# Shifting the start of matmul operand tiles by 128 to 416 bytes in a two-layer hybrid decoder kernel

## The chip, the cores and the metric

The kernel runs on one core of a Trainium2 chip, as one launch. The metric is the device time of that launch in microseconds (us). Three runs of the kernel before gave 1892.44 us as their median, with 1891.72 and 1893.65 us as the ends.

## What is computed

256 tokens of width 1024 go through two layers and a final norm. In short:

```python
for l in range(2):
    sh1, sc1, g1, sh2, sc2, g2 = split(silu(c) @ w_ada[l] + b_ada[l], 6)
    h = rms_norm(x) * (1 + sc1) + sh1
    A, B, C, gates = split(h @ w_in[l])
    m = sig(gA) * (delta_net(A) @ PA) + sig(gB) * (ssd(B) @ PB) + sig(gC) * (mla(C) @ PC)
    x = x + g1 * (m @ w_out[l])
    h = rms_norm(x) * (1 + sc2) + sh2
    f = swiglu(h) if l == 0 else top2_of_8_experts(h)      # experts: 1024 -> 3584 -> 1024
    x = x + g2 * f
out = rms_norm(x) * final_norm_w
```

All weights and activations are float32.

## The kernel before

**Precision.** Every large product is made from three fp32r matmuls. A 1 MB block of weights arrives in a `raw` tile by one DMA on SP's queue (`load_raw`, L145 to L149). `chunk` (L160 to L180) splits it: ScalarE copies it to `whi` in fp32r (L170), VectorE subtracts to get the rest, `wlo` (L172). Activations are split in the same way into a high and a low part. `mm3` (L98) then issues high times high, high times low and low times high, each through `mm`, whose one line (L96) all of these matmuls carry in the profile.

In a row such as `mmt<-whi,xx` the first name behind the arrow is the moving operand (512 columns of weights, streamed) and the second the stationary one (a 128 by 128 block of activations, loaded into the array by the LDWEIGHTS of the same pair). Where a row reads `hh,whi` the two have changed parts.

**The weight ring.** `ring` (L151) hands out `whi` and `wlo` tiles of 4 KB per partition, four of each, in the pool `wp`.

**The stages.** First the mixer of layer 0 (L533 on), then the dense SwiGLU of layer 0 (L1222 on), the mixer of layer 1, and the expert stage of layer 1 (`moe`, L1310 on). Pools of a stage are opened when it begins and take the space that the stage before has left:

- `mx` holds the mixer's small tensors and 16 tiles of 2 KB (`wg`, L539 and L540, tag `w2k`). The delta rule's matrices are there, and in the output product one of the two weight halves, split into `ohi` and `olo` (the second job of `tmajor_gemms` at the end of `mixer`), and in layer 1 the half `qhi`, `qlo` of the query projection.
- `mo`, `mr` and `me` belong to the expert stage. `choose` (L1498) writes the selection matrices `Pm` into `mo`, two buffers. `gather` (L1507) multiplies the tokens `h2` by `Pm` and splits the outcome into `xx`, one tile for two experts in `me` (`[P, 2, 2, KD, P]`: expert, high or low, block of 128 features, 128 tokens). `expert` (L1551) uses it.

**One expert.** Each of the eight experts has 128 slots. `expert` runs seven blocks of 512 hidden columns: the gate product and the up product, each 8 feature blocks times 3 matmuls, so 48 matmuls of 512 columns with `xx` stationary. A block's gate and up are multiplied, turned by four transposes (`trt<-cst,sg`, L1566) and split into `act` (L1549 in the profile, since `behind` issues it). Then 14 chunks of the down weights follow, each with 12 matmuls with `act` stationary, and every second expert has the gather for the next pair in between (32 matmuls `trt<-Pm,h`). The expert's output is scaled, split into `yh` and `yl` (the latter named `sg`) and sent back to the tokens by `outer` (L1589): 8 matmuls with the transposed selection `PTm` as stationary operand, added to `xs` by VectorE (L1607). `outer` is issued two steps later, inside the next expert's first block.

**What sets the order.** The source order, and `behind`/`issue_after`, which places an instruction behind a named one in its engine's queue. Waits come from the tiles: a DMA into `raw` waits for the `wlo` subtraction that read it last, `whi` waits for the matmuls that read that ring slot last, `wlo` for `whi`, and the matmuls for both.

Of the kernel before, what the change touches and what calls it, by code (L numbers as in the profile page):

```python
# [10 lines left out]
F32 = mybir.dt.float32  # L11
# [8 lines left out]
P = 128  # L20
# [41 lines left out]
def trunk_kernel(ctx, tc, a, out, dbg=None):  # L62
# [38 lines left out]
        mm(o, ll, rh, False, stop)  # L101

    nsm = [0]

    def small(w, name, dt=F32, bufs=2):
        return cp.tile([P, w], dt, name=name, tag=name, bufs=bufs)
# [38 lines left out]
    def load_raw(src, k, n, raw=None):  # L145

        raw = raw_tile() if raw is None else raw
        last["load"] = nc.sync.dma_start(raw[:, :k * n], src)
        return raw  # L149
# [383 lines left out]
    def mixer(l, after=None):  # L533

        with tc.tile_pool(name=f"mx{l}", bufs=1, reuse_waits="tile") as mp, \
                tc.tile_pool(name=f"mb{l}", bufs=1, reuse_waits="tile", side="right") as bp, \
                tc.tile_pool(name=f"mc{l}", bufs=1, reuse_waits="tile", side="right") as qp:

            def wg(name, dt=F32):  # L539
                return mp.tile([P, 512], dt, name=name, tag="w2k", bufs=16)  # L540
# [769 lines left out]
    def moe(l):  # L1310
        with tc.tile_pool(name=f"mw{l}", bufs=1, reuse_waits="tile", side="right") as xp, \
                tc.tile_pool(name=f"mo{l}", bufs=1, reuse_waits="tile") as mp:
            for i in range(6):
                xp.tile([P, 2048], F32, name="raw", tag=f"rx{i}")

            extra.update(order=[(xp, f"rx{i}", 1) for i in (3, 4)] + [own] * 2 + [(xp, f"rx{i}", 1) for i in (2, 0, 1, 5)] + [own])
            turn[0] = 0
            ahead.extend(load_raw(w, 4, 512, shot(xp, i, "raw")) for i, w in enumerate(first_srcs[3:7]))
            ahead.extend(load_raw(w, 4, 512) for w in first_srcs[7:15])
            h2 = [mp.tile([P, NT, D], F32R, name="h2", tag="h2", bufs=2) for _ in range(2)]  # L1320
            slot = mp.tile([P, NT, NE], F32, name="slot")
            wsel = mp.tile([P, NT, NE], F32, name="wsel")
            sel = mp.tile([P, NT, NE], F32, name="sel")
            ovi = mp.tile([P, 4], I32, name="ovi")
            ovs = mp.tile([P, 3, 2, NT], F32, name="ovs")
            with tc.tile_pool(name=f"mr{l}", bufs=1, reuse_waits="tile") as rp, \
                    tc.tile_pool(name=f"me{l}", bufs=1, reuse_waits="tile") as ep:
                rest, weights = route(l, rp, h2, slot, wsel, sel)
                pair = lambda e: choose(mp, [lambda t, i=i: slot[:, t, i:i + 1] for i in (e, e + 1)])
                Pm = pair(0)  # L1330
                behind("Pm", rest)
                ready = [(x, Pm, i) for i, x in enumerate(gather(l, ep, h2, Pm, 2, True))]
                behind("xl", weights)
                late = {16: 2, 17: 3, 27: 3}
                ahead.extend(load_raw(first_srcs[i], 4, 512, shot(xp, late[i], "raw") if i in late else None)
                             for i in range(15, 28))
                row_tile[l, 5] = lambda: mp.tile([P, 512], F32, name="g2", tag="g2", bufs=2)
                ada_rows(l, 5)
                g2 = [rows[l, 10 + c] for c in range(2)]

                def after_first(c):
                    if c == 1:
                        with tc.issue_after(last["act"].ins), tc.issue_after(last["tr"].ins):
                            overflow_data(ep, slot, wsel, sel, ovi, ovs)
                def finish():

                    fw, o, f = (raw_tile() for _ in range(3))
                    nc.sync.dma_start(fw[:, :D], a["final_w"])
                    o, f = (x.rearrange("p (t n) -> p t n", t=NT) for x in (o, f))
                    for t in range(NT):  # L1350
                        rs = rms_scale(t, lambda c: o[:, t, c * 512:(c + 1) * 512])
                        for c in range(2):
                            cs = slice(c * 512, (c + 1) * 512)
                            G.tensor_mul(f[:, t, cs], xs[:, t, cs], fw[:, cs])
                        for c in range(2):
                            cs = slice(c * 512, (c + 1) * 512)
                            if c:
                                V.tensor_scalar(o[:, t, cs], f[:, t, cs], rs, None, op0=OP.mult)
                            else:
                                A.activation(o[:, t, cs], f[:, t, cs], AF.Copy, scale=rs)  # L1360
                            nc.sync.dma_start(out[t * P:(t + 1) * P, cs], o[:, t, cs])

                for e in range(NE):
                    x, Pm, i = ready.pop(0)

                    def between():
                        Pm = behind("lo", pair, e + 1)
                        ready.extend((x, Pm, i) for i, x in enumerate(gather(l, ep, h2, Pm, 2)))
                    expert(l, e, ep, xp, x, lambda t, Pm=Pm, i=i: Pm[:, t, i], lambda t, e=e: wsel[:, t, e:e + 1], g2,
                           after_first if e == 0 else None, between if e % 2 and e < NE - 1 else None)  # L1370
                stages.flush()
                finish()
                overflow(l, mp, ep, xp, h2, g2, ovi, ovs, finish)
            extra.clear()

# [37 lines left out]
    def route(l, rp, h2, slot, wsel, sel):  # L1413


        iota = cst[:, C_IOTA:C_IOTA + P]
        lgs, rs = routed["lgs"], routed["rs"]
        tap("logits", lgs)
        halves = [(t, slice(c * 512, (c + 1) * 512)) for c in range(2) for t in range(NT)]
        for t, cs in halves:  # L1420
            A.activation(h2[0][:, t, cs], xs[:, t, cs], AF.Copy, scale=rs[t])
        m8 = rp.tile([P, NT, 8], F32, name="m8")
        i8 = rp.tile([P, NT, 8], U32, name="i8")
        for t in range(NT):
            V.max(m8[:, t], lgs[:, t])
        for t in range(NT):
            V.max_index(i8[:, t], m8[:, t], lgs[:, t])
        i2 = rp.tile([P, NT, 2], F32, name="i2")
        V.tensor_copy(i2, i8[:, :, :2])
        oh = rp.tile([P, NT, 2, NE], F32, name="oh")  # L1430
        V.tensor_tensor(oh.rearrange("p t j n -> p (t j) n"), iota[:, :NE].unsqueeze(1).to_broadcast([P, 2 * NT, NE]),
                        bc(i2.rearrange("p t j -> p (t j)"), NE), op=OP.is_equal)
        chosen = V.tensor_add(sel, oh[:, :, 0], oh[:, :, 1])
        ps = sstile()
        mm(ps[:, 0:NE], cst[:, C_SU:C_SU + P], sel[:, 0], True, True)
        mm(ps[:, NE:2 * NE], cst[:, C_SU:C_SU + P], sel[:, 1], True, False)
        ins = mm(ps[:, NE:2 * NE], ones, sel[:, 0], False, True)
        with tc.issue_after(ins.ins):
            warm(pre[0][0][0], RWARM[2], mmtile)
        V.scalar_tensor_tensor(slot.rearrange("p t n -> p (t n)"), ps[:, :2 * NE], 1.0,  # L1440
                               sel.rearrange("p t n -> p (t n)"), op0=OP.add, op1=OP.mult)

        def low(i):
            t, cs = halves[i]
            V.scalar_tensor_tensor(h2[1][:, t, cs], xs[:, t, cs], rs[t], h2[0][:, t, cs].bitcast(F32), op0=OP.mult,
                                   op1=OP.subtract)
        with tc.issue_after(last["xs"].ins):
            low(0)
        with tc.issue_after(chosen.ins):
            low(1)  # L1450

        def rest():
            low(2)
            low(3)

        def weights():
            e2 = rp.tile([P, NT], F32, name="e2")
            V.tensor_sub(e2, m8[:, :, 1], m8[:, :, 0])
            A.activation(e2, e2, AF.Exp)
            w = rp.tile([P, 2, NT], F32, name="w")  # L1460
            V.tensor_scalar(w[:, 0], e2, 1.0, None, op0=OP.add)
            V.reciprocal(w[:, 0], w[:, 0])
            V.tensor_mul(w[:, 1], e2, w[:, 0])
            for t in range(NT):
                V.tensor_scalar(wsel[:, t], oh[:, t, 0], w[:, 0, t:t + 1], None, op0=OP.mult)
                V.scalar_tensor_tensor(wsel[:, t], oh[:, t, 1], w[:, 1, t:t + 1], wsel[:, t], op0=OP.mult, op1=OP.add)
        return rest, weights
# [328 lines left out]
```

## Time and profile before

| | |
|---|---|
| median of three runs | 1892.44 us (1891.72 to 1893.65) |
| the profiled execution | 1891.01 us |
| its span, first to last instruction | 1889.2 us |
| TensorE (PE) busy | 1841.5 us, 97% |
| VectorE (DVE) busy | 1602.2 us, 85% |
| ScalarE (ACT) busy | 1231.6 us, 65% |
| DMA, mean over the span | 281 GB/s |
| instructions | 25651 |

The profiled execution is one more run, 1.43 us under the median of the three. Its span leaves out 1.8 us of start and end. Matmuls are pipelined: a 512-column one is shown as lasting about 0.39 us although the next starts about 0.23 us later, so what one costs the engine is read from the distance between starts, not from its own length.

### The profile page before, as it was taken

The page shows a single profiled execution, that of the slowest core. Times are in us where ns is not written, and L with a number is a line of the kernel's source. Part 1 is how long each engine was busy: PE and PEld are TensorE (multiplying, and loading weights), DVE is VectorE, ACT ScalarE, POOL GpSimd, SP SyncE. Part 2 cuts the span into 40 slices and gives each one's busy share as a digit, 9 for nine tenths or more (in the row PEclk, how much of TensorE's full clock was granted, in tenths as well). Part 3 has the DMA queues.
Part 4 walks back from the last instruction along what each step waited for, and adds up shares of the span by engine and source line. Part 5 has one row for each costly group of instructions (what it writes and reads, how often), then busy time and mean ns, then how long its engine had stood idle before and what let it go on. Part 6 is the DMA issues. An engine that isn't in the chain of part 4 may idle for free.

```text
span 1889.2 us, 25651 instructions
## 1 busy us (share of the span) xinstructions
PE 1841.5 (97%) x9490; PEld 1545.4 (82%) x9490; DVE 1602.2 (85%) x2313; ACT 1231.6 (65%) x1599; POOL 43.3 (2%) x61
## 2 busy tenths in 40 slices
PE   8999999999999999999999999999999999999996
PEld 6899887788889998888887878878778888788785
DVE  7998788777578978877999989998898999899997
ACT  4665445644466644457777777777877777777775
POOL 0000010000000000100000000000000000000001
PEclk9999999999999999999999999999999999999998
DMA  9453457677644654758998989999899999899892
GB/s 365 160 202 131 171 198 270 235 257 263 211 144 148 221 184 173 276 204 357 340 354 331 356 313 362 363 359 349 331 352 344 354 363 367 307 357 378 336 353 84
DMA packets 75016, 530.19 MB, mean 281 GB/s; under 512 B 8578, under 2 KB 8962, under 8 KB 12548
## 3 DMA queue, kind: packets, MB, share of 16 engines
q1 hardware_dynamic: 74884, 528.49, 74.1%
q8 instruction: 76, 1.25, 0.3%
q14 instruction: 56, 0.46, 0.1%
HBM read 527.41 MB, written 1.05 MB: 280 GB/s over the span
## 4 chain that ended last, share of the span: by engine, by line
PE 87%; DVE 6%; ACT 3%; issue 2%; DMA 2%; DVEq 0%; ACTq 0%; SPq 0%
PE mmt L96 76%; PE smt L96 6%; DVE wlo L172 2%; PE sst L96 2%; PE trt L1566 1%; DVE raw L199 1%; ACT whi L170 1%; PE trt L258 1%; ACT sg L1527 1%; DMA raw<-in_ffn_w_down_dram 0%; PE trt L1073 0%; PE trt L96 0%; DMA raw<-in_w_ada_pair_dram 0%; DMA raw<-in_w_out_dram 0%; DMA raw<-in_w_ada_gate_dram 0%
## 5 line engine op out<-in xcount | busy, mean ns | idle before, releaser
L172 DVE TENSOR_TENSOR wlo<-raw,whi 128x1024 fp32r<-128x1024 f32 (+1 forms) x874 | 1043.7, 1223 | 128.1 <-ACT whi L170 107.1
L170 ACT ACTIVATE whi<-raw 128x1024 fp32r<-128x1024 f32 (+1 forms) x874 | 908.2, 1059 | 305.2 <-PE mmt L96 253.4
L96 PE MATMUL mmt<-whi,xx 128*128 128x512 f32 x1792 | 579.0, 398 | 0.0
L96 PEld LDWEIGHTS mmt<-whi,xx 128*128 128x128 f32 x1792 | 337.4, 188 | 75.0
L96 PE MATMUL mmt<-wlo,xx 128*128 128x512 f32 x896 | 357.6, 399 | 4.9 <-DVE wlo L172 4.9
L96 PE MATMUL mmt<-whi,act 128*128 128x512 f32 x896 | 281.0, 391 | 1.2 <-ACT whi L170 1.2
L96 PEld LDWEIGHTS mmt<-wlo,xx 128*128 128x128 f32 x896 | 168.8, 188 | 52.3 <-DVE wlo L172 16.4
L96 PEld LDWEIGHTS mmt<-whi,act 128*128 128x128 f32 x896 | 167.5, 188 | 36.4 <-ACT whi L170 2.5
L96 PE MATMUL mmt<-whi,hh 128*128 128x512 f32 (+2 forms) x480 | 184.0, 389 | 5.8 <-ACT hh L292 2.0
L96 PE MATMUL mmt<-whi,hl 128*128 128x512 f32 (+2 forms) x480 | 181.1, 383 | 0.5 <-DVE hl L293 0.5
L96 PE MATMUL mmt<-wlo,hh 128*128 128x512 f32 (+2 forms) x480 | 181.2, 383 | 0.0
L96 PE MATMUL mmt<-wlo,act 128*128 128x512 f32 x448 | 175.3, 391 | 1.8 <-DVE wlo L172 1.6
L199 DVE CUSTOM_DVE_ANT_0 raw<-raw,sc_b,pv 128x1024 f32<-128x1024 f32 x96 | 123.2, 1298 | 12.8 <-DMA raw<-in_w_ada_pair_dram 9.8
L96 PEld LDWEIGHTS mmt<-whi,hh 128*128 128x128 f32 x480 | 91.0, 190 | 23.7 <-ACT hh L292 2.6
L96 PEld LDWEIGHTS mmt<-whi,hl 128*128 128x128 f32 x480 | 90.7, 189 | 18.0 <-DVE hl L293 1.0
L96 PEld LDWEIGHTS mmt<-wlo,hh 128*128 128x128 f32 x480 | 90.9, 189 | 16.2 <-DVE wlo L172 0.2
L96 PEld LDWEIGHTS mmt<-wlo,act 128*128 128x128 f32 x448 | 84.1, 188 | 22.3 <-DVE wlo L172 4.4
L96 PE MATMUL mmt<-hh,whi 128*128 128x256 f32 x320 | 92.3, 290 | 0.5 <-ACT whi L170 0.5
L96 PE MATMUL mmt<-hh,wlo 128*128 128x256 f32 x320 | 90.6, 287 | 1.1 <-DVE wlo L172 1.1
L96 PE MATMUL mmt<-hl,whi 128*128 128x256 f32 x320 | 91.0, 285 | 0.0
L1549 ACT ACTIVATE act<-trt 128x512 fp32r<-128x512 f32 x56 | 33.1, 591 | 72.0 <-PE trt L1566 72.0
L1549 DVE TENSOR_TENSOR act<-trt,act 128x512 fp32r<-128x512 f32 x56 | 38.6, 689 | 33.2 <-ACT act L1549 32.7
(422 smaller groups left out, 2226.9 us busy)
## 6 DMA issues: line engine op xcount, KB each, us to landing
raw<-in_moe_w_gate_dram SPq DMA_DIRECT2D x112, 1024.0 KB, 6.0
raw<-in_moe_w_up_dram SPq DMA_DIRECT2D x112, 1024.0 KB, 6.2
raw<-in_moe_w_down_dram SPq DMA_DIRECT2D x112, 1024.0 KB, 6.9
raw<-in_w_in_dram SPq DMA_DIRECT2D x50, 1024.0 KB, 4.9
raw<-in_w_ada_pair_dram SPq DMA_DIRECT2D x32, 1024.0 KB, 5.0
raw<-in_w_ada_gate_dram SPq DMA_DIRECT2D x16, 1024.0 KB, 4.9
raw<-in_ffn_w_down_dram SPq DMA_DIRECT2D x11, 1024.0 KB, 5.5
raw<-in_ffn_w_gate_dram SPq DMA_DIRECT2D x10, 1024.0 KB, 4.9
```

Of the source, the lines that this page charges most:

```text
L96: return T.matmul(o, l, r, start=start, stop=stop, skip_group_check=True)
L170: last["hi"] = A.activation(hi[:, :m], r, AF.Copy)
L172: last["lo"] = V.tensor_sub(lo[:, :m], r, hi[:, :m].bitcast(F32))
L199: last["ada"] = V.tensor_tensor_reduce(r, r, sc_b, 1.0, pv[l][:, PP_BADA + i:PP_BADA + i + 1], OP.mult, OP.add, modc[l][:, i:i + 1])
L258: T.transpose(ps[:, j * S + t * P:j * S + (t + 1) * P], src(t, b0 + j), ident)
L1527: A.activation(tmp[:, o], ps[:, o], AF.Identity, scale=sc, bias=sh)
L1549: return trace(*args, **kw)
L1566: last["tr"] = T.transpose(ps[:, b * P:(b + 1) * P], sg[:, b * P:(b + 1) * P], ident)
```

## The change

Nothing is computed differently. A helper `gap(pool, n)` takes a tile of n bytes per partition that nobody writes or reads, and so moves whatever the pool places behind it:

```diff
+    def gap(pool, n):
+
+        pool.tile([P, n // 4], F32, name="gap", tag=f"gap{n}")
...
         with tc.tile_pool(name=f"mx{l}", bufs=1, reuse_waits="tile") as mp, \
                 tc.tile_pool(name=f"mb{l}", bufs=1, reuse_waits="tile", side="right") as bp, \
                 tc.tile_pool(name=f"mc{l}", bufs=1, reuse_waits="tile", side="right") as qp:
+
+            gap(mp, 128)
...
             ovs = mp.tile([P, 3, 2, NT], F32, name="ovs")
+            gap(mp, 224)
             with tc.tile_pool(name=f"mr{l}", bufs=1, reuse_waits="tile") as rp, \
                     tc.tile_pool(name=f"me{l}", bufs=1, reuse_waits="tile") as ep:
+                gap(ep, 160)
...
                             overflow_data(ep, slot, wsel, sel, ovi, ovs)
+                            gap(ep, 32)
```

Every engine has the same instructions in the same order with the same waits as before; only addresses differ. Where tiles begin in a partition (first buffer in bytes, and what is left modulo 256, which all buffers of a tile share):

| tile | pool | before | left | after | left |
|---|---|---|---|---|---|
| `whi`, `wlo` ring | `wp` | 59872, 76256 | 224 | the same | 224 |
| `hh`, `hl` (in the expert stage `h2`) | `hp`, `mo` | 92640, 100832 | 224 | the same | 224 |
| `act` | `mw` | 196576 | 224 | the same | 224 |
| `yh`, `yl` of the mixers | `mb` | 182240, 181216 | 224 | the same | 224 |
| mixers' 2 KB tiles (`ohi`, `olo`, `qhi`, `qlo`, the delta rule's) | `mx` | 113760 | 96 | 113888 | 224 |
| `Pm` | `mo` | 109312 | 0 | 109536 | 224 |
| `xx` | `me` | 117856 | 96 | 118240 | 224 |
| `sg` | `me` | 134240 | 96 | 134624 | 224 |
| `PTm` | `me` | 140384 | 96 | 140768 | 224 |
| `yh` of the experts | `me` | 142656 | 64 | 143072 | 224 |

The blocks that a matmul reads inside these tiles lie at multiples of 512 bytes from their start, so what is left modulo 256 holds for each of them too.

## Rows read from the trace of the kernel before

**Rows 1.** The page, busy time of the engines: us, share of the span, instructions.
```profile
PE 1841.5 (97%) x9490; PEld 1545.4 (82%) x9490; DVE 1602.2 (85%) x2313; ACT 1231.6 (65%) x1599; POOL 43.3 (2%) x61
```

**Rows 2.** The page, the chain that ended last, by engine and line.
```profile
PE mmt L96 76%; PE smt L96 6%; DVE wlo L172 2%; PE sst L96 2%; PE trt L1566 1%; DVE raw L199 1%; ACT whi L170 1%; PE trt L258 1%; ACT sg L1527 1%; DMA raw<-in_ffn_w_down_dram 0%; PE trt L1073 0%; PE trt L96 0%; DMA raw<-in_w_ada_pair_dram 0%; DMA raw<-in_w_out_dram 0%; DMA raw<-in_w_ada_gate_dram 0%
```

**Rows 3.** Stretches: the expert stage; length, PE, PEld, DVE, ACT, POOL busy, clock, DMA share, GB/s.
```profile
866.00:1869.00 1003.00, 995.12 (x4475) 805.09 (x4474) 908.17 (x929) 768.91 (x839) 2.29 (x7) 1.00 0.89 341
```

**Rows 4.** Line L96 on PE: count, shortest/median/longest ns, first and last start, forms.
```profile
L96 PE MATMUL mmt<-whi,xx x1792: 387/393/483, 865.8 to 1830.6; 128*128 128x512 f32 x200
L96 PE MATMUL mmt<-wlo,xx x896: 387/393/505, 866.1 to 1830.4; 128*128 128x512 f32 x180
L96 PE MATMUL mmt<-whi,act x896: 387/389/499, 949.7 to 1869.2; 128*128 128x512 f32 x180
...
L96 PE MATMUL mmt<-whi,yh x96: 387/389/481, 217.6 to 824.2; 128*128 128x512 f32 x96
```

**Rows 5.** Timeline of PE, one gate and up block: start, us, line, operation, tiles.
```profile
1402.33 0.40 PE L96 MATMUL mmt<-wlo,xx 128*128 128x512 f32 x1
...
1413.03 0.40 PE L96 MATMUL mmt<-whi,xx 128*128 128x512 f32 x1
```

**Rows 6.** Timeline of PE, one stretch of the down product.
```profile
1340.20 0.39 PE L96 MATMUL mmt<-whi,act 128*128 128x512 f32 x1
...
1349.72 0.39 PE L96 MATMUL mmt<-whi,act 128*128 128x512 f32 x1
```

**Rows 7.** Timeline of PE, output product of layer 1's mixer: second half, then first half.
```profile
834.85 0.40 PE L96 MATMUL mmt<-ohi,hl 128*128 128x512 f32 x1
...
839.04 0.40 PE L96 MATMUL mmt<-ohi,hl 128*128 128x512 f32 x1
...
840.21 0.39 PE L96 MATMUL mmt<-wlo,hh 128*128 128x512 f32 x1
...
843.84 0.39 PE L96 MATMUL mmt<-whi,hl 128*128 128x512 f32 x1
```

**Rows 8.** Timeline of PE, 256-column matmuls: a mixer's projection, and a gather.
```profile
560.09 0.28 PE L96 MATMUL mmt<-hh,wlo 128*128 128x256 f32 x1
...
561.53 0.28 PE L96 MATMUL mmt<-hh,wlo 128*128 128x256 f32 x1
...
1355.84 3.90 PE L96 MATMUL trt<-Pm,h 128*128 128x256 f32 x32
1359.58 0.39 PE L96 MATMUL mmt<-whi,act 128*128 128x512 f32 x1
```

**Rows 9.** Waits in the expert stage (866 to 1869): us in total, times, longest.
```profile
ACT whi L170 <- PE mmt L96: 131.7, 396, 2.7
ACT act L1549 <- PE trt L1566: 72.0, 36, 2.2
...
PEld mmt L96 <- DVE wlo L172: 20.9, 44, 1.1
...
SPq L148 <- DVE wlo L172: 806.9, 309, 9.1
```

**Rows 10.** Timeline of PE at the change from one expert to the next.
```profile
1369.64 0.40 PE L96 MATMUL mmt<-whi,xx 128*128 128x512 f32 x1
...
1381.94 0.50 PE L96 MATMUL mmt<-wlo,xx 128*128 128x512 f32 x1 [0.78 <-DVE wlo L172]
```

**Rows 11.** Timelines of PE and PEld around one late `wlo` inside a block.
```profile
1425.57 0.40 PE L96 MATMUL mmt<-wlo,xx 128*128 128x512 f32 x1
...
1428.40 0.19 PEld L96 LDWEIGHTS mmt<-wlo,xx 128*128 128x128 f32 x1 [0.30 <-DVE wlo L172]
```

**Rows 12.** Timeline of DVE: a split of `xx`, and work of one block.
```profile
1365.36 0.68 DVE L1533 TENSOR_TENSOR xx<-sg,xx 128x512 fp32r<-128x512 f32 x1
...
1388.48 3.49 DVE L172 TENSOR_TENSOR wlo<-raw,whi 128x1024 fp32r<-128x1024 f32 x3
1391.89 0.68 DVE L1549 TENSOR_TENSOR act<-trt,act 128x512 fp32r<-128x512 f32 x1
```

## The prediction

> **What bounds the kernel now.** I read the busy times first: TensorE (PE) is busy 97% of the span [rows 1], and matmuls of line L96 into `mmt` alone are 76% of the chain that ended last [rows 2]. So what a matmul costs PE counts, unless something else is late where it gets cheaper. [...]
>
> The view of line L96 by tiles shows what the change is about. The same `whi` and `wlo` ring is the moving operand in all four rows of that group, and all are 512 columns wide. With `act` or the mixers' `yh` stationary the median is 389 ns, with `xx` 393 [rows 4]. Of the four stationary tiles `xx` alone begins at another place modulo 256 than the ring (96 against 224).
>
> Since matmuls overlap, the price is the distance between starts. In one gate and up block the starts from 1402.33 to 1413.03 are 46 distances: 10.70/46 = **232.6 ns** [rows 5]. In the down product 42 distances fill 1340.20 to 1349.72: 9.52/42 = **226.7 ns** [rows 6]. The difference is 5.9 ns.
>
> That could belong to the stage and not to the place. The output product of a mixer is the control: same line, same stationary `hh` and `hl`, same PSUM use, a few us apart, and only the moving tile differs. With `ohi` and `olo` (place 96) 18 distances take 839.04 - 834.85 = 4.19 us, 232.8 ns each. With the ring (224) 16 take 843.84 - 840.21 = 3.63 us, 226.9 ns each [rows 7]. The same 5.9 ns, with the roles of the two operands exchanged. So the place of the operands matters. That it is the place modulo 256 is my reading: the dearer tiles also lie in one stretch of the partition, 113760 to 147 thousand, and the trace has no tile there at 224 that could tell the two apart.
>
> **The change part by part.** No instruction, order or wait changes, so the whole effect must come from durations.
>
> *`xx` from 96 to 224.* There are 1792 + 896 = 2688 matmuls with `xx` [rows 4]. No row shows `xx` at 224. Its price then lies between 226.7, the price with `act` at 224 in the same stage, and 232.6, no change; I take 226.7, because `act` has the same size, the same moving tiles and the same stage. Gross gain: 2688 x 5.9 ns = **15.9 us**. The worse end, a price above 232.6, is a rival below.
>
> *What of it is absorbed.* PE does not run alone. Two waits end at a time that other engines set, and PE only reaches them earlier.
> - Change of expert. DVE is behind after scaling and adding the previous output, and PE stands 0.78 us for `wlo`, having started 39 `xx` matmuls since 1369.64 [rows 10]. Their 39 x 5.9 ns = 0.23 us goes into that wait. There are seven such changes: 1.6 us.
> - Inside blocks. ACT, once it is ahead, waits in order for the four transposes, 36 times in the stage; its copies and DVE's next `wlo` come late from there, and PE's weight load waits for `wlo` 44 times [rows 9]. Such a wait ends at 1428.40, and the first matmul after the one behind the transposes began at 1425.57, 12 distances before [rows 11]. This chain has a fixed length, so 12 x 5.9 ns = 0.07 us is lost each time: 44 x 0.07 = 3.1 us.
>
> Net for `xx`: 15.9 - 1.6 - 3.1 = **11.2 us**. Where the stalls go, the late thing is always the next `wlo`. DVE can follow: three `wlo` take 1391.89 - 1388.48 = 3.41 us, 1.14 us each [rows 12], so a block of eight with two smaller operations of at most 0.68 costs DVE 8 x 1.14 + 2 x 0.68 = 10.5 us, while PE needs 48 x 226.7 ns = 10.9 us for the matmuls alone.
>
> *Mixers' 2 KB tiles from 96 to 224.* Those with 512 columns on PE are `ohi`/`olo` (48 matmuls in layer 0, 24 in layer 1) and `qhi`/`qlo` (24): 96 x 5.9 ns = **0.6 us** gained, all on PE's path at most, and nothing as the other end. The delta rule's tiles have 64 or 128 columns and were both at 96 already; for them, as for the transposes, I count nothing.
>
> *`PTm` and `yh` of the experts.* 64 matmuls, 64 x 5.9 ns = 0.4 us at most. They run in the stretch before the wait at the change of expert [rows 10], which covers them: **0**. If that cover is gone, 0.4 us more is gained.
>
> *`Pm` from 0 to 224.* Here the nearest rows speak against the change. 32 gather matmuls of 256 columns, `Pm` moving at 0 and `h2` stationary at 224, take 1359.58 - 1355.84 = 3.74 us, 116.9 ns each. The mixer's 256-column matmuls with both at 224 take (561.53 - 560.09)/12 = 120.0 ns [rows 8]. So the four gathers, 128 matmuls, may cost 128 x 3.1 ns = **0.4 us more**; the other end is nothing.
>
> *ACT and DVE on moved tiles.* DVE's split into `xx` (96) takes 0.68 us and its split into `act` (224) also 0.68 [rows 12]. I count nothing.
>
> *DMA.* No transfer moves. SP's queue waits 309 times for DVE to free a `raw` tile [rows 9], and no wait for weights from memory stands among that stage's longer ones, so the transfers are ahead of the work. At a DMA share of 0.89 [rows 3], a stage shorter by 1.1% raises it to 0.90.
>
> **Sum.** -11.2 - 0.6 + 0.4 = -11.4 us on the profiled execution's 1891.01, so 1879.6. The median of the runs, 1892.44, is 1.43 above the profiled one; by the same difference I predict **1881.0 us**. The bounds of the terms: all 15.9 arrives, with 0.6 and 0.4 on top, gives 1892.44 - 16.9 = 1875.5; the other way, twice as much absorbed (9.4) and nothing from the mixers, 1892.44 - 6.5 + 0.4 = 1886.3. A measurement of this kernel can tell 0.2%, 3.8 us, from no change.
>
> **The rivals.**
>
> *The late `wlo` takes it all in most blocks* (chance 0.08). Where ACT already waits for the transposes, the chain from there to `wlo` sets the pace of the whole block. Then 36 of 56 blocks [rows 9] gain nothing: 36 x 48 x 5.9 ns = 10.2 us lost instead of 3.1. 15.9 - 1.6 - 10.2 = 4.1 us remain, 1888.3. Against it: only 12 of the 48 distances lie between the transposes and the late `wlo` [rows 11], and ACT waits for PE to free ring tiles 396 times [rows 9], so most splits are ready early.
>
> *The place modulo 256 does nothing* (0.14): **1892.4**. The cause would be the stretch of the partition in which these pools lie, which the gaps leave as it is. For it: all tiles at the price of 232.6 are there. Against it: those at 226.7 lie below it (ring, `hh`) and far above (`act`, `yh`), which leaves no simple rule by distance. [...]
>
> *Equal places are worse* (0.04), the slower side. If two streams that begin at the same place modulo 256 met in the same piece of memory, moving `xx` onto the ring's place would add what the gathers suggest, 3.1 ns per matmul [rows 8]: 2688 x 3.1 = 8.3 us, **1900.7**. It decides against the change once the distance with `xx` exceeds 232.6 + 3.8/2.688 = 234.0 ns. Against it: ring and `act`, ring and `hh` are such equal pairs and cost 227 ns [rows 6, 7].
>
> **How the numbers follow.** The forecast, full effect with some absorbed, has 0.74. With 0.08, 0.14 and 0.04 the chances add to 1. The forecast's bounds, 1875.5 to 1886.3, and the absorbed case, 1888.3, make up 0.82; I let the range run from 1875 to 1889 and leave the other two out. Faster by over 3.8 us means below 1888.6: nearly all of the first two cases, 0.81. Within 3.8 us: the no-effect case and a remainder of the absorbed one, 0.15. Slower: 0.04.
>
> **What would show it.** Right, if the medians with `xx` fall from 393 to 389 ns and the distances to about 227 ns, those of `ohi` too, while `act` stays at 226.7; if PE's weight loads wait longer for `wlo`, by some 5 us in all; and if the expert stage ends 11 us earlier with the 866 us before it shortened by under 1 us. Gather distances near 120 ns would show the small loss. Wrong, if `xx` stays at 232.6 (the place is not it, or not this remainder), or if it falls to 227 and the stage still takes 1003 us: then the waits for `wlo` have grown by the whole 15.9 us, and DVE or ACT is the bound.

## The result, and the profile after

The changed kernel takes **1879.91 us** (median of 8 runs, 1878.59 to 1887.58) beside 1892.41 us for the kernel before (8 runs, 1889.61 to 1897.14): a ratio of 0.9939, 95% interval 0.9925 to 0.9953, so 0.6% faster. The forecast was 1881.0 us, with a range of 1875 to 1889. The profiled execution took 1882.09 us over a span of 1880.3, 2.2 us above its median.

The page, busy time of the engines, to be held against [rows 1]:

```profile
PE 1832.1 (97%) x9490; PEld 1545.1 (82%) x9490; DVE 1600.5 (85%) x2313; ACT 1231.8 (66%) x1599; POOL 42.1 (2%) x61
```

The counts are the same for every engine. PE's busy time fell by 9.4 us, that of no other engine by more than 1.7. The expert stage, same columns as [rows 3]:

```profile
866.00:1860.00 994.00, 986.42 (x4491) 805.73 (x4491) 908.02 (x931) 770.00 (x841) 2.26 (x7) 1.00 0.90 345
```

The granted clock of the stage is 1.00, as before; the DMA share went from 0.89 to 0.90. PE is still the engine that is busy nearly throughout. By tiles of line L96, the rows that answer to [rows 4], with the output product of the mixers and the `PTm` product below (count, shortest/median/longest ns, first and last start, forms):

```profile
L96 PE MATMUL mmt<-whi,xx x1792: 387/389/481, 868.0 to 1821.9; 128*128 128x512 f32 x200
L96 PE MATMUL mmt<-wlo,xx x896: 387/389/507, 868.2 to 1821.7; 128*128 128x512 f32 x180
L96 PE MATMUL mmt<-whi,act x896: 387/389/501, 950.2 to 1860.5; 128*128 128x512 f32 x180
...
L96 PE MATMUL mmt<-ohi,hh x40: 278/389/481, 314.6 to 854.1; 128*128 128x512 f32 x24, 128*128 128x256 f32 x16
...
L96 PE MATMUL smt<-yh,PTm x32: 389/389/501, 995.8 to 1864.1; 128*128 128x512 f32 x32
```

`xx` has come down from 393 to the 389 that `act` kept. From the first `xx` start to the last `act` start the stage takes 1860.5 - 868.0 = **992.5 us**, where it took 1869.2 - 865.8 = 1003.4 [rows 4]: 10.9 us less, of the 12.5 by which the medians differ.

The first 866 us say nothing at this size. In the profiled executions of this document (e2 left out, where the ring moves in the mixers too) the stage starts anywhere from 863.6 to 868.0: at 868.0 in the change and at 864.0 in the run e6 below, two kernels that issue the same work from the same places up to the gather just before it. Most of these 4.0 us come with the granted clock. Between the 2800th and the 3000th matmul (509 to 556 us) the lead of e6 grows from 1.2 to 4.0 us, and from 542 to 550 us the clock of the change is 0.57 on the mean, with 0.50 in each us from 543 to 549, where e6 has 1.00 over the whole. It had fallen by 543.27, when PE had stood idle for 2.03 us; e6, some 1.2 us ahead there, shows no fall from 542 to 550. The stretch first in the change, then in e6, columns as above:

```profile
542.00:550.00 8.00, 6.73 (x22) 6.11 (x23) 4.44 (x7) 7.71 (x16) 0.00 (x0) 0.57 0.00 1
...
542.00:550.00 8.00, 7.89 (x42) 7.13 (x43) 5.59 (x8) 7.30 (x14) 0.00 (x0) 1.00 0.00 0
```

The timeline of PE in one gate and up block shows that the new price is not one number (start, us, line, operation, tiles):

```profile
1400.96 0.39 PE L96 MATMUL mmt<-wlo,xx 128*128 128x512 f32 x1
...
1408.44 0.39 PE L96 MATMUL mmt<-wlo,xx 128*128 128x512 f32 x1
1408.67 0.39 PE L96 MATMUL mmt<-whi,xx 128*128 128x512 f32 x1
1408.90 0.60 PE L1576 MATMUL trt<-cst,sg 128*128 128x128 f32 x4
1409.26 0.48 PE L96 MATMUL mmt<-whi,xx 128*128 128x512 f32 x1
1409.57 0.40 PE L96 MATMUL mmt<-wlo,xx 128*128 128x512 f32 x1
...
1411.65 0.39 PE L96 MATMUL mmt<-wlo,xx 128*128 128x512 f32 x1
1411.88 0.61 PE L96 MATMUL mmt<-whi,xx 128*128 128x512 f32 x2
1412.33 0.39 PE L96 MATMUL mmt<-wlo,xx 128*128 128x512 f32 x1
```

From 1400.96 to 1408.44 there are 33 distances between starts, 7.48/33 = 226.7 ns, exactly the price of `act`. Behind the four transposes, from 1409.57 to 1411.65, there are nine, 2.08/9 = **231.1 ns**; then the 226.7 comes back. Before the change there was no such step: the block of [rows 5] began right behind transposes too, and its mean is 232.6 over the whole of it.

The longer waits of the stage (us in total, times, longest), to be held against [rows 9] (the added lines move L170 and L172 to L174 and L176):

```profile
ACT whi L174 <- PE mmt L96: 124.7, 389, 2.7
ACT act L1559 <- PE trt L1576: 70.1, 36, 2.1
...
PEld mmt L96 <- DVE wlo L176: 21.7, 45, 1.1
```

PE's weight loads waited 20.9 us for `wlo` before, and 21.7 now. Over all PE starts of the stage, those 2562 distances from an `xx` matmul to the next start that are under 245 ns (which leaves out the stalls and the first distance behind the transposes) had a mean of 232.6 ns before, 595.9 us in sum; now 2559 have 228.2 ns and 584.0 us. The longer ones went from 126 with 45.3 us to 129 with 46.7 us; three distances have crossed the 245 ns, which puts 0.7 us into both differences. So `xx` gives -11.9 + 1.4 us; `PTm` gives -0.3, stalls in the down product -0.3, the rest +0.2.

### The profile page after: what moved, and what is told of

The parts are those of the page before. It is cut to its first block, busy times and chain, and to the rows that moved or that the text cites. A ratio compares the mean times of both kernels' runs of the same rounds, so it can differ in the third digit from the quotient of the medians.

```text
span 1880.3 us, 25651 instructions
## 1 busy us (share of the span) xinstructions
PE 1832.1 (97%) x9490; PEld 1545.1 (82%) x9490; DVE 1600.5 (85%) x2313; ACT 1231.8 (66%) x1599; POOL 42.1 (2%) x61
## 4 chain that ended last, share of the span: by engine, by line
PE 87%; DVE 6%; ACT 3%; issue 2%; DMA 2%; SPq 0%; DVEq 0%; ACTq 0%
PE mmt L96 76%; PE smt L96 6%; DVE wlo L176 2%; PE sst L96 2%; PE trt L1576 1%; DVE raw L203 1%; ACT whi L174 1%; PE trt L262 1%; DMA raw<-in_w_ada_pair_dram 1%; ACT sg L1537 1%; PE trt L1079 0%; PE trt L96 0%; DMA raw<-in_w_out_dram 0%; DMA pv<-in_params_dram 0%; DMA raw<-in_w_ada_gate_dram 0%
## 5 line engine op out<-in xcount | busy, mean ns | idle before, releaser
L176 DVE TENSOR_TENSOR wlo<-raw,whi 128x1024 fp32r<-128x1024 f32 (+1 forms) x874 | 1042.0, 1223 | 125.4 <-ACT whi L174 102.0
L174 ACT ACTIVATE whi<-raw 128x1024 fp32r<-128x1024 f32 (+1 forms) x874 | 908.2, 1059 | 296.5 <-PE mmt L96 248.5
L96 PE MATMUL mmt<-whi,xx 128*128 128x512 f32 x1792 | 571.5, 393 | 0.0
L96 PEld LDWEIGHTS mmt<-whi,xx 128*128 128x128 f32 x1792 | 336.5, 188 | 68.2
L96 PE MATMUL mmt<-wlo,xx 128*128 128x512 f32 x896 | 353.8, 395 | 4.9 <-DVE wlo L176 4.7
L96 PE MATMUL mmt<-whi,act 128*128 128x512 f32 x896 | 280.9, 391 | 0.9 <-ACT whi L174 0.9
L96 PEld LDWEIGHTS mmt<-wlo,xx 128*128 128x128 f32 x896 | 168.4, 188 | 50.5 <-DVE wlo L176 17.3
L96 PEld LDWEIGHTS mmt<-whi,act 128*128 128x128 f32 x896 | 167.5, 188 | 36.1 <-ACT whi L174 2.2
L96 PE MATMUL mmt<-whi,hh 128*128 128x512 f32 (+2 forms) x480 | 184.3, 389 | 5.7 <-ACT hh L296 2.0
L96 PE MATMUL mmt<-whi,hl 128*128 128x512 f32 (+2 forms) x480 | 181.4, 383 | 0.5 <-DVE hl L297 0.5
L96 PE MATMUL mmt<-wlo,hh 128*128 128x512 f32 (+2 forms) x480 | 181.3, 383 | 0.0
L96 PE MATMUL mmt<-wlo,act 128*128 128x512 f32 x448 | 175.2, 391 | 1.8 <-DVE wlo L176 1.6
L96 PEld LDWEIGHTS mmt<-whi,hh 128*128 128x128 f32 x480 | 91.2, 190 | 23.6 <-ACT hh L296 2.6
L96 PEld LDWEIGHTS mmt<-whi,hl 128*128 128x128 f32 x480 | 90.9, 189 | 18.0 <-DVE hl L297 1.0
L96 PEld LDWEIGHTS mmt<-wlo,hh 128*128 128x128 f32 x480 | 91.1, 190 | 16.2 <-DVE wlo L176 0.2
L96 PEld LDWEIGHTS mmt<-wlo,act 128*128 128x128 f32 x448 | 84.1, 188 | 22.2 <-DVE wlo L176 4.4
L96 PE MATMUL mmt<-hh,whi 128*128 128x256 f32 x320 | 92.4, 290 | 0.4 <-ACT whi L174 0.4
L96 PE MATMUL mmt<-hh,wlo 128*128 128x256 f32 x320 | 90.6, 287 | 1.2 <-DVE wlo L176 1.1
L96 PE MATMUL mmt<-hl,whi 128*128 128x256 f32 x320 | 91.0, 285 | 0.0
```

The costliest lines, as they stand in the source:

```text
L96: return T.matmul(o, l, r, start=start, stop=stop, skip_group_check=True)
L174: last["hi"] = A.activation(hi[:, :m], r, AF.Copy)
L176: last["lo"] = V.tensor_sub(lo[:, :m], r, hi[:, :m].bitcast(F32))
```

## The experiments

What the first four are to tell apart is *why* the place of `xx` matters: because it equals the ring's place modulo 256 (the forecast's reading), because 224 itself is a good place, or because of the region of the partition in which the tile lies. The kernel before ran 13 times beside them, median 1891.08 us.

**e1: `xx` at another place in every expert.** The kernel before, with the eight experts' `xx` at 96, 128, 160, 192, 224, 0, 32 and 64 in turn, in the same region.

```diff
+    gathers = [0]
...
-        xx = ep.tile([P, 2, 2, KD, P], F32R, name="xx", tag="xx")
+        big = ep.tile([P, 4160], F32R, name="xx", tag="xx")
+        off = 16 * (gathers[0] % 4)
+        gathers[0] += 1
+        xx = big[:, off:off + 4112].rearrange("p (e x) -> p e x", e=2)[:, :, :2048]
+        xx = xx.rearrange("p e (i k n) -> p e i k n", i=2, k=KD)
```

> The kernel before, with the eight experts' `xx` at eight places: 96, 128, 160, 192, 224, 0, 32, 64 modulo 256, expert by expert; the ring stays at 224. Theory A (what counts is that moving and stationary operand begin at the same place modulo 256): the distance between starts is 227 ns for the fifth expert alone and 229 to 233 for the seven others. Theory B (the stretch of the partition, not the place): all eight stay at 232.6 ns, since all lie where `xx` lay before. A third way: the distance depends on the difference in steps, with a second good place, which would have to be next to 224 (192 or 0), since 96 and, for `ohi`, 96 are known to be bad.

Matmuls with `xx`, experts at 96, 160, 224 and 0 (columns as above):

```profile
L96 PE MATMUL mmt<-whi,xx x224: 390/393/483, 863.7 to 947.3; 128*128 128x512 f32 x112
...
L96 PE MATMUL mmt<-whi,xx x224: 388/392/483, 1115.1 to 1198.8; 128*128 128x512 f32 x112
...
L96 PE MATMUL mmt<-whi,xx x224: 387/389/481, 1367.0 to 1450.4; 128*128 128x512 f32 x112
...
L96 PE MATMUL mmt<-whi,xx x224: 389/396/482, 1489.2 to 1574.1; 128*128 128x512 f32 x112
```

Mean distances under 245 ns by place: 96: 232.7; 128: 233.4; 160: 229.4; 192: 233.2; 224: **228.3**; 0: 233.1; 32: 233.2; 64: 233.8. One run took 1887.65 us. The region is out: the same region holds prices from 228.3 to 233.8. Nor is it the order of the experts: with one place for all, the eight means are 232.5 to 232.8 in the kernel before and 227.9 to 228.5 in the change. Nor is it `sg` or `PTm`, which e3 and e4 below move along with `xx`: here they stay at 96. The addresses also decide that 256 is the step to count in. The places 96 and 224 are the same modulo 128 and cost 232.7 and 228.3; the tile at 224 begins at 117984 here and at 118240 in the change, not the same modulo 512, and costs 228 both times. That 160 stands in between was in no theory.

**e2: the ring moved instead of `xx`.** The kernel before, with the ring's tiles put at 96 by 128 bytes left free. Now ring and `xx` are equal at 96, while `act`, `hh` and `yh` stay at 224 and have become the unequal ones.

```diff
+    shifted = []
...
-        return tuple(pool.tile([P, 1024], F32R, name=nm, tag=nm + x, bufs=bufs) for nm in ("whi", "wlo"))
+        if not shifted:
+            wp.tile([P, 32], F32, name="gap", tag="gapa", bufs=1)
+        t = tuple(pool.tile([P, 1024], F32R, name=nm, tag=nm + x, bufs=bufs) for nm in ("whi", "wlo"))
+        if not shifted:
+            wp.tile([P, 32], F32, name="gap", tag="gapb", bufs=1)
+            shifted.append(1)
+        return t
```

> The kernel before, with the weight ring moved to 96 and all else left at its remainder (`xx` 96, `act`, `hh`, `yh` 224, `ohi` 96). Theory A1 (equal places are good, whichever they are): `xx` falls from 232.6 to 227 or 228 ns, `act` rises from 226.7 to about 232.6; in all -11 us for `xx`, +8 us for the 1344 matmuls with `act`, and some +5 to +10 us for those with `hh`, `yh` and `ah`, so 1894 to 1900 us. Theory A2 (224 itself is the good place, for each operand by itself): `xx` stays at or above 232.6 and `act` rises, 1905 us or more. Theory B (stretch of the partition): nothing changes, 1892 us.

Line L96 by tiles in this kernel:

```profile
L96 PE MATMUL mmt<-whi,xx x1792: 387/389/482, 871.5 to 1831.2; 128*128 128x512 f32 x200
...
L96 PE MATMUL mmt<-whi,act x896: 387/393/502, 953.9 to 1870.7; 128*128 128x512 f32 x180
...
L96 PE MATMUL mmt<-whi,yh x96: 390/393/483, 217.6 to 829.8; 128*128 128x512 f32 x96
```

The two prices have changed sides: `xx`, not moved itself, falls from 393 to 389, `act` and `yh`, not moved either, rise from 389 to 393. So neither the tile's own place nor 224 counts, but how the two operands stand to each other. The mean distances are 228.1 with `xx` and 232.5 with `act` (227.3 in the kernel before). In the stage that makes 2688 x 4.5 = 12.1 us gained and 1344 x 5.2 = 7.0 lost; the stage took 999.2 us, 4.2 less. The one run took 1892.19 us, under the 1894 to 1900 put down for A1. It is 1.1 us above the 1891.08 of the kernel before, where 2 to 7 more were expected, and a single run can't settle so little: the rows decide here, not the time.

**e3: the 128 bytes for `xx` alone.** The kernel before with one gap. `xx`, and with it `sg` and `PTm`, go to 224; `Pm`, the mixers' tiles and the experts' `yh` stay where they were or miss the ring's place.

```diff
+                ep.tile([P, 32], F32, name="gap", tag="gap128")
                 rest, weights = route(l, rp, h2, slot, wsel, sel)
```

> The kernel before with one gap of 128 bytes ahead of the expert pool: `xx`, `sg` and `PTm` go to 224, while `Pm` (0), the mixers' tiles (96) and the experts' `yh` (192) stay apart from it. If `xx` carries the change, the time is 10 to 11 us under the kernel before (1881 to 1882), within 1.5 us of the change as a whole. If the mixers' tiles carry more than the 0.6 us counted, it stays further above the change.

It took 1881.76 us (4 runs, 1880.3 to 1882.84), ratio 0.9953, 0.9936 to 0.997. The rows:

```profile
L96 PE MATMUL mmt<-whi,xx x1792: 387/389/482, 866.6 to 1820.8; 128*128 128x512 f32 x200
...
L96 PE MATMUL mmt<-whi,act x896: 387/389/497, 948.9 to 1859.3; 128*128 128x512 f32 x180
```

Its stage is 1859.3 - 866.6 = 992.7 us, against the change's 992.5.

**e4: the change without `xx`.** The changed kernel with the pool's two gaps exchanged, so that `xx`, `sg` and `PTm` are back at 96 and all else stays moved.

```diff
-                gap(ep, 160)
+                gap(ep, 32)
...
-                            gap(ep, 32)
+                            gap(ep, 160)
```

> The changed kernel with `xx`, `sg` and `PTm` put back to 96, all other gaps kept. If `xx` carries the change, nearly all of it goes: 1891 to 1892 us, at most 1.5 us under the kernel before. If the other gaps carry a part, it stays between.

```profile
L96 PE MATMUL mmt<-whi,xx x1792: 387/393/483, 867.8 to 1832.8; 128*128 128x512 f32 x200
...
L96 PE MATMUL mmt<-whi,act x896: 387/389/504, 951.7 to 1871.4; 128*128 128x512 f32 x180
```

1891.04 us (10 runs), ratio 0.9998, 0.9989 to 1.0008; the stage takes 1003.6 us, as before. With e3 this makes one statement from two sides: `xx` carries the gain, and everything else that the change moves is worth less than these runs can tell. (`sg` and `PTm` move along with `xx` in both; e1 has shown the price of `xx` without them.)

**e5: what slows the matmuls behind the transposes?** The transposes move the identity in `cst` at 128, so the slower stretch could be left behind by another unequal pair (theory C). Or any interruption of the row of equal matmuls brings it (theory D). The changed kernel with `cst` at 224:

```diff
+    cp.tile([P, 24], F32, name="gap", tag="gapa")
     cst = cp.tile([P, NCST], F32, name="cst")
+    cp.tile([P, 40], F32, name="gap", tag="gapb")
```

> The changed kernel with the table `cst`, whose identity block moves in every transpose, shifted from 128 to 224 modulo 256; all other tiles keep their remainder. In the changed kernel some ten distances behind each batch of transposes with `sg` are 231.5 ns before 227 returns, so the mean with `xx` is 228.2. Theory C (the unequal place of the transposes' two operands leaves the two streams out of step): those ten fall to 227, the mean with `xx` to about 227.0, and 2560 x 1.2 ns = 3 us of the expert stage's 992.5 go, a third of it perhaps into the waits for `wlo`: 1877 to 1879 us. Theory D (any pause or change of length puts them out of step, whatever the place): the mean stays at 228.2 and the time at 1880.

The timeline of PE in this kernel, behind one batch of transposes:

```profile
1404.48 0.60 PE L1578 MATMUL trt<-cst,sg 128*128 128x128 f32 x4
1404.83 0.48 PE L98 MATMUL mmt<-whi,xx 128*128 128x512 f32 x1
1405.14 0.40 PE L98 MATMUL mmt<-wlo,xx 128*128 128x512 f32 x1
...
1407.23 0.39 PE L98 MATMUL mmt<-wlo,xx 128*128 128x512 f32 x1
1407.46 0.62 PE L98 MATMUL mmt<-whi,xx 128*128 128x512 f32 x2
1407.91 0.39 PE L98 MATMUL mmt<-wlo,xx 128*128 128x512 f32 x1
```

Nine distances in 2.09 us, 232.2 ns, then three in 0.68 us, 226.7: the stretch is still there, and the mean with `xx` is 228.0. C falls. D fits: in the change a late `wlo` brings such a stretch too, with means of 231.5 to 234.9 ns for the first four distances behind it and 227.3 to 230.9 for the next six. Why, no run shows. 1878.43 us (4 runs), ratio to the kernel before (1892.33, 7 runs) 0.9932, 0.9916 to 0.9949, which these runs don't tell from the change.

**e6: `Pm` back at 0.** The changed kernel; `g2` and six small tiles of the routing go back with `Pm`, all else stays in its place:

```diff
-            gap(mp, 224)
...
-                gap(ep, 160)
+                gap(ep, 384)
```

> The changed kernel with `Pm` put back to 0, all else at the same addresses. The gather's distance falls from 119.8 to 117 ns (the small loss that was predicted is real): 128 x 3 ns = 0.4 us, too little to see in the time, 1879.5 to 1880 us apart from the spread of single runs. If it stays at 120, the 117 ns before had another cause than the place.

The distance in the second, third and fourth gather went back from 119.8 to 116.8 ns, which is what it was before; their durations (the median was 283 in the change):

```profile
L96 PE MATMUL trt<-Pm,h x128: 277/280/356, 860.0 to 1602.1; 128*128 128x256 f32 x128
```

128 x 3.0 ns = 0.4 us. The one run, 1878.06 us, can't show so little. For these matmuls of 256 columns the equal place is the dearer one. e2 has a second such pair, `lh` moving and `wlo` stationary: 119.9 ns with both at 224, 118.7 with the ring at 96.

**e7: places close to the ring's.** As e1, with the experts' `xx` at 208, 216, 220, 228, 232, 240, 216 and 224.

```diff
-        off = 16 * (gathers[0] % 4)
+        off = (28, 31, 34, 30)[gathers[0] % 4]
```

(The tile is 4136 long, and the step from one expert's half to the other's 4100 instead of 4112. `sg` and `PTm` behind it come to lie at 0.)

> The kernel before, with the eight experts' `xx` at 208, 216, 220, 228, 232, 240, 216 and 224 modulo 256, so from 16 bytes below to 16 bytes above the ring's place. If the two operands must start at the same place to the byte, the last expert alone has a mean of about 228 ns between starts and the others 232 or more. If only the same line of 16 or 32 bytes counts (224 to 239, or 224 to 255), those at 228 and 232 have 228 too, with 240 in or out, and those below 224 have 232 or more. If nearness counts, all eight lie between 227 and 230, lowest at 224.

Matmuls with `xx`, experts at 208, the first 216, 232 and 224:

```profile
L96 PE MATMUL mmt<-whi,xx x224: 387/389/497, 863.9 to 948.2; 128*128 128x512 f32 x112
...
L96 PE MATMUL mmt<-whi,xx x224: 388/396/482, 987.0 to 1071.0; 128*128 128x512 f32 x112
...
L96 PE MATMUL mmt<-whi,xx x224: 387/392/506, 1367.9 to 1452.1; 128*128 128x512 f32 x112
...
L96 PE MATMUL mmt<-whi,xx x224: 387/389/482, 1744.0 to 1827.6; 128*128 128x512 f32 x112
```

Mean distances: 208: **227.7**; 216: 233.3; 220: 231.9; 228: 232.4; 232: 230.8; 240: 232.9; 216 again: 233.3; 224: 228.4. One run took 1887.73 us, beside 1892.25 for the kernel before. None of the three pictures that I had of the neighbourhood fits. The equal place is cheap each time, but 16 bytes below it is as cheap, while 8 bytes below costs the full 5 ns and 8 above about half of that. At 512 columns equality is sufficient in what was tried, not necessary; I found no rule for the 14 places, and why a place is cheap stays open.

No version here is clearly faster than the change: e5 and e6 lie 1.5 and 1.9 us below its median and 0.2 and 0.5 below its lowest run, and the intervals of the ratios of e5 and the change overlap.

## Why the prediction was right, and where its terms were off

- **What bounds.** Right. PE's counts stayed, its matmuls got cheaper, and the stage's end followed.
- **Place modulo 256, not the region.** Right, and now shown by e1 and e2; the forecast had it as a reading with a rival of 0.14 ([rows 4], from which it starts, has three stationary tiles, not four). The times speak against that rival too: weight load and moving operand are the same tiles with the same counts in e3 and e4, in the same stretch of the partition, and only their places differ, yet the stages take 992.7 and 1003.6 us. The reading was too tidy all the same: one other place, 208, is as cheap as the equal one (e7), and 160 stands between (e1).
- **`xx`, gross 15.9 us.** The step that failed in size: "I take 226.7, because `act` has the same size, the same moving tiles and the same stage". The distances with `xx` have a mean of 228.2, and the gross gain is 11.9 us. The 226.7 is reached only in the steady part. After every batch of transposes nine distances stay near 231, and behind a late `wlo` some ten stay near 231 as well. By these means (an estimate) the 48 batches with `xx` right behind them hold 48 x 9 x 4.4 ns = 1.9 us of the 4.0 that are missing, and 32 late `wlo` 32 x 10 x 4.1 ns = 1.3.
- **Absorbed, 4.7 us.** Also off, and in one half the step itself was wrong. The long distances grew by 1.4 us, half of which is the three that crossed 245 ns; the waits for `wlo` grew by 0.8 us in all, not by some 5. *Change of expert*, 1.6 us forecast: nothing was absorbed. The wait in the trace before, then the same change in the changed kernel:

```profile
1380.07 0.69 DVE L1607 TENSOR_TENSOR xs<-xs,smt 128x512 f32<-128x512 f32 x1 [0.51 <-PE smt L96]
1380.67 2.35 DVE L172 TENSOR_TENSOR wlo<-raw,whi 128x1024 fp32r<-128x1024 f32 x2
1381.94 0.50 PE L96 MATMUL mmt<-wlo,xx 128*128 128x512 f32 x1 [0.78 <-DVE wlo L172]
...
1376.27 0.69 DVE L1617 TENSOR_TENSOR xs<-xs,smt 128x512 f32<-128x512 f32 x1 [0.30 <-PE smt L96]
1376.88 2.35 DVE L176 TENSOR_TENSOR wlo<-raw,whi 128x1024 fp32r<-128x1024 f32 x2
1378.15 0.51 PE L96 MATMUL mmt<-wlo,xx 128*128 128x512 f32 x1 [0.78 <-DVE wlo L176]
```

  I had taken the end of this wait for a time that DVE sets. But the late `wlo` stands on DVE right behind an addition to `xs`, and that addition waits for PE's own `PTm` product (0.51 us before, 0.30 after). When PE comes earlier, so does the `wlo`, and the 0.78 us stay. There are six such waits, not seven, 1.10 us each on the side of the weight load, all unchanged, and 38 `xx` matmuls stand before each, not 39. *Inside blocks*, 3.1 us forecast: the mechanism held, but its numbers didn't. Of the 44 waits only 25 end 12 distances behind the transposes. PE came not 12 x 5.9 = 71 ns earlier to them but some 31 ns, since nine of the 12 distances gained 232.6 - 231.1 = 1.5 ns and only three 5.9. These 25 waits grew from about 0.30 to 0.33 us, 0.5 us in all. So what was not gained behind the transposes could not be absorbed there, and this part of both misses has one cause. That the rest of them nearly cancels is luck: the net is 10.5 us against 11.2 forecast, and the sum came out better than its parts.
- **Mixers' 2 KB tiles, -0.6 us.** The price is right: the `ohi`/`olo` distances of layer 1 in the changed kernel are

```profile
837.04 0.39 PE L96 MATMUL mmt<-ohi,hl 128*128 128x512 f32 x1
...
841.12 0.39 PE L96 MATMUL mmt<-ohi,hl 128*128 128x512 f32 x1
```

  18 in 4.08 us, 226.7 ns, where [rows 7] had 232.8. That the 0.6 us arrive at the end is not shown; they are smaller than the 4 us by which the start of the stage varies.
- **`PTm` and `yh`, 0.** They gained 0.3 us, near the other end of 0.4: the cover that I named did not hold them, for the same reason as at the change of expert. This part is too small to see in a time.
- **`Pm`, +0.4 us.** Right to the tenth: 116.9 before, 119.8 after, 116.8 in e6.
- **ACT, DVE, DMA, 0.** DVE's busy time in the stage is 908.02 us against 908.17, ACT's 770.00 against 768.91; the DMA share is the forecast 0.90.
- **The rivals.** A late `wlo` that takes it all: no, the wait grew by 0.8 us, not by 10. Equal places worse: no for 512 columns; yes for 256, where it costs the 0.4 us above.

## What to carry to other kernels

Where one line of matmuls shows two medians for the same shape, sort the rows by the operands' places modulo 256 bytes: here a free 128 bytes in one pool were worth 0.5% (e3, ratio 0.9953, 0.9936 to 0.997). Try the place with a scan inside one run, as e1 does, and judge it by distances between starts, since a few ns each may not show in one run's time (in e6 128 x 3.0 ns didn't). Take the price of a new place from the stretches in which it will run, those behind an interruption included (231.1 ns behind transposes here, 226.7 further on). Before a wait is counted as absorbing a gain, look what the late work itself waits for: where that is the engine that gets faster, the wait may stay as it is (0.78 us before and after here).

## What the runs showed of the hardware

- Back-to-back matmuls of 512 columns with a weight load each cost 226.7 ns with `act` and 232.6 with `xx` in one stage at a granted clock of 1.00, by how the places of the moving and the stationary tile stand to each other: with the ring moved by 128 bytes the means are 228.1 ns with `xx` and 232.5 with `act`, where they had been 232.6 and 227.3 (e2).
- The cheap distance is not there at once: nine distances behind four transposes have a mean of 231.1 ns with the transposes' identity at 128 and of 232.2 at 224 (e5), and only then 226.7.
- Close to the cheap place the price is not smooth: 0 and 16 bytes below cost 228.4 and 227.7 ns, 8 bytes below 233.3 and 8 above 230.8 (e7).
- For 256 columns the order is reversed for the pairs tried: 116.8 ns with the moving tile at 0 and the stationary at 224, 119.8 with both at 224 (e6); 118.7 with 224 and 96, 119.9 with both at 224 (e2).
